# Two weight tiles of each SwiGLU's second product, loaded some steps of the program sooner

## The chip, the cores and the metric

The kernel runs on one core of a Trainium2 chip. The metric is the device time of one execution in microseconds (us), shown as the median of three runs. Engines are named as the profile names them: PE is the matrix engine (PEld its weight loads), DVE the vector engine, ACT the scalar engine, SP the engine that issues nearly all DMAs here, in one queue and in order. A DMA that waits on SP holds back all DMAs behind it.

## What is computed

One layer of an encoder on x of 1024 tokens by 1024 features, all float32:

```
h = x + 0.5 * SwiGLU_1(RMSNorm(x))                 # SwiGLU(u) = (silu(u W_gate) * (u W_up)) W_out
u = RMSNorm(h); [q|k|v|g|p|gates] = u W_in         # retention branch and pooling branch
h = h + (sum of gated branches) W_o
h = h + 0.5 * SwiGLU_2(RMSNorm(h))
out = RMSNorm(h)
```

Each SwiGLU has 2816 hidden features. Its first product (to gate and up) and its second (W_out) stand back to back; the change lies where the second begins. There are two such places, one for each SwiGLU.

## The kernel before

**Arithmetic.** Each float32 operand is split in two rounded parts (L161 on ACT makes the high part, L162 on DVE the rest), and each product is three matmuls (`mm3`, L181 to L183). On top of that both SwiGLU products run as Strassen products over 2x2 blocks: seven block products instead of eight, with sums and differences of blocks made on DVE.

**Names.** `ffn_in` is the first product: tiles named a in SwiGLU 1 and c in SwiGLU 2. `a_ra` and `a_rb` are raw weights, `a_S`, `a_wS`, `a_wL`, `a_wx` and the like are combinations of them and their split forms, `a_a`, `a_b`, `a_e`, `a_x`, `a_y` are PSUM banks, `ag` and `au` the gate and up tiles. `ffn_out` is the second product: tiles named b in SwiGLU 1 and d in SwiGLU 2. It runs over k = 0 to 10, pairs of hidden blocks. For each k its first step p1(k) loads `r` (hidden rows that the first product stored, shown as `br<-r`), `ra` (a 512 KB row of W_out, shown as `bra<-in_f_out`) and for two k at a time the block `bL22a`. Step p6(k) makes three sums of weight blocks on DVE: `s1 = L21 + L22` (L906), `s2 = s1 - L11` (L907), `s3 = L11 - L21` (L908). All three read `ra`.

**Order of the work.** The kernel is one stream of steps, each a preparation (loads and splits) and a body (matmuls). `Flow.run` calls a step's preparation four steps (`LOOK`) ahead of its body. Work that has no place of its own (scaling by the norm, silu, stores of hidden tiles) goes into a queue, `flow.back`; after each body the next one or two pieces of that queue are taken (`flow.rate`). A scheduler under this then sets each engine's order. So while the last two groups of `ffn_in` are still on PE, the first steps of `ffn_out` already stand among them on DVE, ACT and SP.

**Buffers.** `ra` for k below 4 comes from `wide`, a pool of 28 buffers ("mv") which also holds the normed input in split form, n1 or n3, the moving operand of `ffn_in`. Such a buffer comes free when the last matmul that reads its operand is done. `ra` for k from 4 comes from `raw`, four buffers shared with the raw weights of `ffn_in`.

**At the end of ffn_in.** The last two groups share part of their seventh of the products through `common` (L576 onwards): `one`, `two` and `three` multiply halves of blocks into the bank `a_x` and others. Before `three` PE must wait for DVE: L619 reads `a_x` into `ag`, and only then may the matmuls of `three` add on to the same bank.

Of the kernel before, what the change touches and what calls it, by code (L numbers as in the profile page):

```python
# [18 lines left out]
S = 1024  # L19
# [34 lines left out]
BY_OPERAND = (0, 4, 1, 3, 2, 6, 5)  # L54
# [36 lines left out]
def block_kernel(ctx: ExitStack, tc, x, x_tok, x_two, vecs, f1_in, f1_out, w_in, w_v, pool_w, w_ret, w_pool, w_o,  # L91
# [25 lines left out]
    def wide(name):  # L117
        return sb.tile([P, S], F32, tag="mv", bufs=N_MV, name=name)
# [4 lines left out]
    def tl(name):  # L123
        return sb.tile([P, S], F32, tag="tl", bufs=N_TL, name=name)
# [4 lines left out]
    def c2(name):  # L129
        return sb.tile([P, H], F32, tag="c2", bufs=N_C2, name=name)  # L130
# [4 lines left out]
    def sum_bank(name):  # L135

        return ps.tile([P, H], F32, tag="sum", bufs=N_SUM, name=name)

    def load(dst, src):
        nc.sync.dma_start(dst, src)  # L140
# [8 lines left out]
    def half(t, j):  # L149
        return t[:, j * H : (j + 1) * H]  # L150
# [67 lines left out]
    for n in range(N_SUM):  # L218
        b = sum_bank(f"set{n}")
# [77 lines left out]
    class Next(Norm):  # L297
# [24 lines left out]
        def g(self, mt, v=None):  # L322
            if self.gain is None:
                return None
            v = vec if v is None else v
            return v[:, self.gain + mt : self.gain + mt + 1]
# [307 lines left out]
    def parted(steps, between):  # L634

        return steps[0], steps[1], between, steps[2]
# [14 lines left out]
    def then(step, work):  # L651


        def body():
            step[1]()
            flow.add(*work)

        return step[0], body

    def pairs_of_both(nx, groups, first, some):  # L660

        groups = list(groups)
        A, B = (g(()) for g in groups[:2])
        steps = [g[m] for m in first for g in (A, B)]
        n = 2
        if len(groups) % 2:
            C = groups[n](())
            steps += [C[m] for m in BY_SUM]
            n += 1
        tl_, t4_ = ("tl", N_TL), ("t4", N_T4)  # L670

        steps[-1] = then(steps[-1], nx.blocks("R22", [t4_, tl_, t4_], True))
        yield from steps
        for k, n in enumerate(range(n, len(groups), 2)):
            A, B = (g((2, 3) if k >= some else (3,)) for g in groups[n : n + 2])
            yield A[0]
            yield B[0]
            if k < some:
                yield A[4]
                yield then(B[4], nx.blocks("R21", [tl_] * 3, True)) if k == some - 1 else B[4]  # L680
            if k > some:
                yield from parted(common(nx, A, B, 2), A[3])
            else:
                yield A[3]
            yield from (A[1], B[3], B[1], A[2], B[2])
            if k != some:
                yield from parted(common(nx, A, B, 3), A[6])
                yield B[6]
            else:
                yield from parted(common(nx, A, B, 2), A[6])  # L690
                yield from parted(common(nx, A, B, 3), B[6])
# [46 lines left out]
            yield prep, body  # L738


    def ffn_in(nx, w, ops, name, start=None):

        R, T, B, T4 = ops
        hid = {}

        def group(g):
            gate_up = {}

            def dest(which):
                tile, j = which  # L750
                if tile not in gate_up:
                    gate_up[tile] = (tl if start and g == 0 else t4)(f"{name}{'gu'[tile]}{g}")
                return half(gate_up[tile], j)

            later = []

            def evac(which, in0, in1):
                tile, j = which
                dst, rms = dest(which), nx.rb
                if in1 is not None:  # L760
                    tt(dst, in0, in1, ADD)
                elif not tile and rms is not None:
                    tt(dst, in0, half(rms, j), MUL)
                    return
                else:
                    copy(dst, in0)
                if not tile:
                    later.append(j)

            def end():  # L770
                gate, up = gate_up[0], gate_up[1]

                def scale():
                    if len(later) == 2:
                        tt(gate, gate, nx.rms(), MUL)
                    else:
                        for j in later:
                            tt(half(gate, j), half(gate, j), half(nx.rms(), j), MUL)

                def times(j):  # L780
                    tt(half(up, j), half(gate, j), half(up, j), MUL)

                flow.add(scale, lambda: act(gate, gate, AF.Silu), lambda: times(0), lambda: times(1))
                hid[g] = up
                k = g % FH
                if g < FH:
                    return
                lo, hi, e = hid.pop(k), up, {}
                R11, R12, R21, R22 = half(lo, 0), half(lo, 1), half(hi, 0), half(hi, 1)

                def w1():

                    e["n"], e["m"] = gate, c2(f"{name}m{k}")
                    tt(half(e["n"], 0), R12, R11, SUB)

                def w1b():
                    tt(half(e["n"], 1), R22, R12, SUB)
                    load(B[k], e["n"])

                def w2():  # L800
                    tt(R12, R22, half(e["n"], 0), SUB)
                    load(R[k], lo)
                    load(T[k], hi)

                def w3():
                    tt(e["m"], R21, R12, SUB)
                    load(T4[k], e["m"])
                    done.add(k)

                flow.add(w1, w1b, w2, w3)  # L810

            if start and g == 0:
                return plain_group(nx, start, f"{name}{g}_", evac, end)
            return lambda shared: strassen(nx, w[g, 0], w[g, 1], f"{name}{g}_", evac, end, shared=shared, dest=dest)

        done = ops_done.setdefault(name, set())
        order = [g for k in range(FH) for g in (k, k + FH)]
        if start:

            return chain(group(0), pairs_of_both(nx, (group(g) for g in order[1:]), BY_OPERAND, 3))  # L820
        return pairs_of_both(nx, (group(g) for g in order), BY_OPERAND, 2)


    def plain_group(nx, blocks, name, evac, end):
# [25 lines left out]
    ops_done = {}  # L850


    def ffn_out(nx, ops, ready, w, res, name, sink, end, last=None, beyond=None):

        R, T, B, T4 = ops
# [3 lines left out]
        def rows():  # L861

            t["rb"] = wide(f"{name}rb")
            act(in_row(t["rb"]), in_turns(nx.rms()), AF.Copy, scale=0.5)
# [24 lines left out]
        def p1(k):  # L889
            flow.until(lambda: k in ready)  # L890
            r = tl(f"{name}r{k}")
            load(r, R[k])
            ra = (wide if k < 4 else raw)(f"{name}ra{k}")
            load(ra, w[k, :, :S])
            if k == 6:
                rows()
                for mt in range(KT):
                    acc[mt] = t4(f"{name}acc{mt}")
            t["x"] = half(ra, 0), half(ra, 1), both("L22a", k, lambda z: w[z, :, 2 * H : 3 * H])
            t["r"] = r  # L900
            return half(ra, 0), half(r, 0)
# [45 lines left out]
        ahead = {}  # L947
# [160 lines left out]
    first = Next("n1", V_FFN1)  # L1108
    xt = {mt: t4(f"x{mt}") for mt in range(KT)}
    ra, rb = raw("ra"), raw("rb")  # L1110
    lead = half(ra, 0), half(ra, 1), half(rb, 0), half(rb, 1)
# [28 lines left out]
    ops1 = spill("r", FH), spill("t", FH), spill("b", FH), spill("m", FH, H)  # L1140
    h1, h2 = spill("h1", KT), spill("h2", KT)
# [3 lines left out]
    gates = spill("gt", 2 * KT)  # L1145
    pm, ret = spill("pm", KT), spill("ret", KT)

    def ffn1():
        for n, step in enumerate(ffn_in(first, f1_in, ops1, "a", lead)):
            flow.rate = 1  # L1150
            yield step
        flow.rate = 2
        yield from ffn_out(first, ops1, ops_done["a"], f1_out, x_two, "b", mix.quarter, end1)

    mix = Next("n2", V_MIX, h1)

# [233 lines left out]
    order = [("q", 0), ("k", 0), *(o for pair in zip(heavy, light) for o in pair), *light[len(heavy) :]]  # L1390
# [472 lines left out]
    ffn2 = Next("n3", V_FFN2, h2)  # L1863
    ops2 = spill("r2", FH), spill("t2", FH), spill("b2", FH), spill("m2", FH, H)
# [90 lines left out]
    fin = Last("n4")  # L1955

    def second():
        for n, step in enumerate(ffn_in(ffn2, f2_in, ops2, "c")):
            flow.rate = 1
            yield step  # L1960
        flow.rate = 2
    flow.run(chain(ffn1(), projections(), retention(), merge(), second(),
                   ffn_out(ffn2, ops2, ops_done.setdefault("c", set()), f2_out, h2, "d", fin.quarter, fin.end, fin, f2_far)))
    flow.some(-1)


# [93 lines left out]
```

## Time and profile before

| | |
|---|---|
| median of 3 runs | 2071.99 us (2071.73 to 2072.92) |
| profiled execution | 2071.6 us, of which the span shown by the profile is 2069.8 us |
| PE busy | 2044.7 us, 99% of the span |
| DVE busy | 1835.8 us, 89% |
| ACT busy | 1091.3 us, 53% |
| granted PE clock | 0.999 of full speed on average |
| DMA | 313.57 MB, mean 151 GB/s |

The span leaves 25.1 us in which PE does nothing. Views of the trace give for each instruction its start, its length, and in brackets the idle time before it on its engine with what ended that idle time. Tile names are shown without their numbers, so which `bra` is meant follows from its place in the row of issues.

### The profile page before, as it was taken

Reading aid. Unit: us, or ns where it says so; the run is one execution under the profiler, and the core shown is the slowest. Engines: PE = TensorE matmul, PEld = TensorE weight load, DVE = VectorE, ACT = ScalarE, POOL = GpSimd, SP = SyncE. Lnnn points to the kernel's source line nnn. Section 1 sums busy time; section 2 is a strip of 40 time slices with the busy share of each in tenths; the row PEclk is TensorE's granted clock in tenths of the full one; section 3 lists DMA queues with packets and bytes.
Section 4 is the critical chain, followed back from the end, with each engine's and each line's share of the span. In section 5 each row is a group of like instructions: output and inputs, shape, how many; then the busy total and the mean of one; then the engine's idle time right before and its main releaser. Section 6 shows DMA issues by size and latency. Waiting matters only on the chain.

```text
span 2069.8 us, 29688 instructions
## 1 busy us (share of the span) xinstructions
PE 2044.7 (99%) x10672; PEld 1811.1 (87%) x10672; DVE 1835.8 (89%) x3262; ACT 1091.3 (53%) x2061; POOL 0.2 (0%) x4
## 2 busy tenths in 40 slices
PE   9999999999999999999999999999999999999998
PEld 7888989888888888888888999888789999988887
DVE  8799898998996798999778888999989989899897
ACT  8545444554654535454447763456645545455454
POOL 0000000000000000000000000000000000000000
PEclk9999999999999999999999999999999999999999
DMA  7232424576542323243337566724224232457642
GB/s 263 82 138 77 143 87 142 200 265 203 179 151 94 120 106 130 91 143 120 119 128 236 188 234 235 253 92 162 72 86 137 91 136 87 134 207 267 216 145 100
DMA packets 118819, 313.57 MB, mean 151 GB/s; under 512 B 13200, under 2 KB 17424, under 8 KB 118672
## 3 DMA queue, kind: packets, MB, share of 16 engines
q1 hardware_dynamic: 118096, 310.64, 44.4%
q8 instruction: 83, 1.36, 0.3%
q10 hardware_dynamic: 576, 1.05, 0.1%
q14 instruction: 64, 0.52, 0.1%
HBM read 220.93 MB, written 90.70 MB: 151 GB/s over the span
## 4 chain that ended last, share of the span: by engine, by line
PE 74%; DVE 18%; issue 3%; DMA 3%; ACT 3%; SPq 0%; ACTq 0%; DVEq 0%
PE c_b L181 2%; PE c_b L182 2%; PE c_b L183 2%; PE a_b L181 2%; PE a_b L182 2%; PE a_b L183 2%; PE c_e L183 1%; PE c_e L182 1%; PE c_e L181 1%; PE a_e L181 1%; PE a_e L182 1%; PE a_e L183 1%; PE dp5a L181 1%; PE dp5a L182 1%; PE dp5a L183 1%
## 5 line engine op out<-in xcount | busy, mean ns | idle before, releaser
L182 PE MATMUL c_b<-n3T,c_wS 128*128 128x512 f32 x176 | 66.8, 380 | 0.0
L181 PE MATMUL c_b<-n3T,c_wS 128*128 128x512 f32 x176 | 66.5, 380 | 0.2 <-ACT n3T L161 0.2
L183 PE MATMUL c_b<-n3T,c_wS 128*128 128x512 f32 x176 | 66.7, 379 | 0.0
L181 PE MATMUL a_b<-n1T,a_wS 128*128 128x512 f32 x168 | 63.7, 379 | 0.0
L182 PE MATMUL a_b<-n1T,a_wS 128*128 128x512 f32 x168 | 63.7, 379 | 0.0
L183 PE MATMUL a_b<-n1T,a_wS 128*128 128x512 f32 x168 | 63.7, 379 | 0.0
L181 PE MATMUL a_a<-n1R,a_wL 128*128 128x512 f32 x120 | 45.5, 379 | 0.0
L182 PE MATMUL a_a<-n1R,a_wL 128*128 128x512 f32 x120 | 45.5, 379 | 0.0
L183 PE MATMUL a_a<-n1R,a_wL 128*128 128x512 f32 x120 | 45.5, 379 | 0.0
L182 PE MATMUL c_a<-n3R,c_wL 128*128 128x512 f32 x112 | 42.7, 381 | 1.1 <-DVE n3R L166 1.1
L181 PE MATMUL c_a<-n3R,c_wL 128*128 128x512 f32 x112 | 42.6, 380 | 0.8 <-ACT c_b L521 0.8
L183 PE MATMUL c_a<-n3R,c_wL 128*128 128x512 f32 x112 | 42.5, 379 | 0.0
L181 PEld LDWEIGHTS c_b<-n3T,c_wS 128*128 128x128 f32 x176 | 33.2, 189 | 5.1 <-ACT n3T L161 0.6
L182 PEld LDWEIGHTS c_b<-n3T,c_wS 128*128 128x128 f32 x176 | 33.3, 189 | 4.8 <-DVE n3T L162 0.3
L183 PEld LDWEIGHTS c_b<-n3T,c_wS 128*128 128x128 f32 x176 | 33.3, 189 | 4.6
L162 DVE TENSOR_TENSOR a_wS<-a_S,a_wS 128x512 fp32r<-128x512 f32 x45 | 31.3, 697 | 5.0 <-ACT a_wS L161 4.9
L183 PEld LDWEIGHTS a_b<-n1T,a_wS 128*128 128x128 f32 x168 | 31.8, 189 | 4.5
L182 PEld LDWEIGHTS a_b<-n1T,a_wS 128*128 128x128 f32 x168 | 31.8, 189 | 4.3
L181 PEld LDWEIGHTS a_b<-n1T,a_wS 128*128 128x128 f32 x168 | 31.8, 189 | 4.4
L162 DVE TENSOR_TENSOR c_wS<-c_S,c_wS 128x512 fp32r<-128x512 f32 x46 | 32.0, 698 | 2.4 <-ACT c_wS L161 2.3
L161 ACT CAST c_wS<-c_S 128x512 fp32r<-128x512 f32 x46 | 27.8, 622 | 11.4 <-DVE c_S L484 7.0
L182 PE MATMUL c_e<-n3T,c_wL 128*128 128x512 f32 x88 | 33.5, 380 | 0.1
(3159 smaller groups left out, 8034.8 us busy)
## 6 DMA issues: line engine op xcount, KB each, us to landing
c_ra<-in_f_in SPq DMA_DIRECT2D x22, 512.0 KB, 3.7
c_rb<-in_f_in SPq DMA_DIRECT2D x22, 512.0 KB, 3.8
a_ra<-in_f_in SPq DMA_DIRECT2D x21, 512.0 KB, 3.9
a_rb<-in_f_in SPq DMA_DIRECT2D x21, 512.0 KB, 3.8
t<-au SPq DMA_DIRECT2D x11, 512.0 KB, 2.8
b<-ag SPq DMA_DIRECT2D x11, 512.0 KB, 3.7
r<-au SPq DMA_DIRECT2D x11, 512.0 KB, 3.5
bra<-in_f_out SPq DMA_DIRECT2D x11, 512.0 KB, 5.8
```

Source lines behind the costliest of these rows:

```text
L161: copy(hi, src)
L162: tt(lo, src, hi.bitcast(F32), SUB)
L181: mm(dst, w[0], m[0], start=start, stop=False, skip_group_check=True)
L182: mm(dst, w[0], m[1], start=False, stop=False, skip_group_check=True)
L183: mm(dst, w[1], m[0], start=False, stop=stop, skip_group_check=True)
```

## The change

The loads of `ra` for k = 0 and k = 1 are taken out of p1 and put into a function `fetch_rows`, which is handed to `ffn_in`. In the last pair of groups it is put into the `flow.back` queue after the body of step `B[3]`, the fourth block product of the second group. Eight more steps of `ffn_in` follow before p1(0) of `ffn_out`. Since preparations run four steps ahead, p1(0)'s loads were called before when four more bodies had run, and those of p1(1), two steps behind it, when six had. The loads of k = 2 and later stay where they were.

```diff
-            yield from (A[1], B[3], B[1], A[2], B[2])
+            yield A[1]
+            yield then(B[3], [ahead]) if n == len(groups) - 2 else B[3]
+            yield from (B[1], A[2], B[2])
...
-            ra = (wide if k < 4 else raw)(f"{name}ra{k}")
-            load(ra, w[k, :, :S])
+            if k < 2:
+                ra = fetched[name, k]
+            else:
+                ra = (wide if k < 4 else raw)(f"{name}ra{k}")
+                load(ra, w[k, :, :S])
...
+    fetched = {}
+
+    def fetch_rows(w, name):
+        for k in range(2):
+            r = fetched[name, k] = wide(f"{name}ra{k}")
+            load(r, w[k, :, :S])
...
-        for n, step in enumerate(ffn_in(first, f1_in, ops1, "a", lead)):
+        for n, step in enumerate(ffn_in(first, f1_in, ops1, "a", lambda: fetch_rows(f1_out, "b"), lead)):
...
-        for n, step in enumerate(ffn_in(ffn2, f2_in, ops2, "c")):
+        for n, step in enumerate(ffn_in(ffn2, f2_in, ops2, "c", lambda: fetch_rows(f2_out, "d"))):
```

What this does to each engine is seen in the order of the built program's instructions, which has no times. In these rows tiles carry their k: `bra1` is `ra` of k = 1, `bs10`, `bs20` and `bs30` hold s1, s2 and s3 of k = 0 and 1. In brackets stand the semaphores waited for: `DMAHW0` to `DMAHW7` count earlier DMAs in turn, `PE`, `DVE` and `Activation` count those engines' work.

SP's queue before, SwiGLU 1, from the store of the hidden rows r9 to the load of `bra4`:

```order
L140 DMA r9_133<-au9_3653 128x1024 [waits DMAHW5_49,DVE_49]
L140 DMA bL22a2_4154<-in_f1_out 128x512 [waits DMAHW6_49,Activation_49]
L140 DMA bL22a2_4154<-in_f1_out 128x512 [waits DMAHW7_49]
L140 DMA m9_166<-am9_3916 128x512 [waits DMAHW0_49,DVE_49]
L140 DMA bra1_4101<-in_f1_out 128x1024 [waits DMAHW1_49]
L140 DMA bra2_4152<-in_f1_out 128x1024 [waits DMAHW2_49,PE_49]
L140 DMA br3_4213<-r3_127 128x1024 [waits DMAHW3_49,DVE_49]
L140 DMA br4_4261<-r4_128 128x1024 [waits DMAHW4_49,DVE_49,Activation_49]
L140 DMA bra4_4263<-in_f1_out 128x1024 [waits DMAHW5_49,Activation_49]
```

Here `bra1` waits for no engine of its own account, only for its turn: it stands twelve DMAs behind `bra0`, right behind the store `m9`, which waits for DVE.

SP's queue after, at the place where `bra0` stands in both programs (the two rows ahead of it are the same in both):

```order
L140 DMA a21_rb_3719<-in_f1_in 128x1024 [waits DMAHW4_49,DVE_49]
L140 DMA bra0_4003<-in_f1_out 128x1024 [waits DMAHW5_49,PE_49]
L140 DMA bra1_4005<-in_f1_out 128x1024 [waits DMAHW6_49,PE_49]
L140 DMA br0_4049<-r0_124 128x1024 [waits DMAHW7_49,PE_49]
L140 DMA t9_144<-au20_3670 128x1024 [waits DMAHW0_49,DVE_49]
L140 DMA bL22a0_4051<-in_f1_out 128x512 [waits DMAHW1_49,DVE_49,Activation_49]
```

`bra0` has not moved on SP: it has the same neighbour ahead and the same PE event to wait for as before. `bra1` now stands right behind it and waits for a PE event, the sixth matmul of that block product where `bra0` waits for the third. Further on in SP's queue after:

```order
L140 DMA m9_166<-am9_3916 128x512 [waits DMAHW1_49,DVE_49]
L140 DMA bra2_4152<-in_f1_out 128x1024 [waits DMAHW2_49,PE_49]
L140 DMA br3_4213<-r3_127 128x1024 [waits DMAHW3_49,DVE_49]
L140 DMA bra4_4263<-in_f1_out 128x1024 [waits DMAHW4_49,DVE_49]
L140 DMA bL22a4_4265<-in_f1_out 128x512 [waits DMAHW5_49,DVE_49]
L140 DMA bL22a4_4265<-in_f1_out 128x512 [waits DMAHW6_49]
L140 DMA br4_4261<-r4_128 128x1024 [waits DMAHW7_49,DVE_49]
L140 DMA br5_4310<-r5_129 128x1024 [waits DMAHW0_49,PE_49]
```

`bra2` has moved up to the place that `bra1` held behind `m9`, and `br4` has moved back by three DMAs, behind `bL22a4`.

DVE before, SwiGLU 1, from the split of `a10_wL22` to L619:

```order
L162 TENSOR_TENSOR a10_wL22_3986<-a10_rb_3698,a10_wL22_3986 128x512
L162 TENSOR_TENSOR bp6m1_4132<-br1_4099,bp6m1_4132 128x512
L906 TENSOR_TENSOR bs10_4072<-bra1_4101,bL22a0_4049 128x512
L761 TENSOR_TENSOR au21_4018<-a21_b_3822,a21_p7_3960 128x512
L162 TENSOR_TENSOR a10_wy3_4003<-a21_S2_3876,a10_wy3_4003 128x256
L907 TENSOR_TENSOR bs20_4073<-bs10_4072,bra1_4101 128x512
L908 TENSOR_TENSOR bs30_4074<-bra1_4101 128x512
L162 TENSOR_TENSOR bp1m2_4160<-br2_4150,bp1m2_4160 128x512
L162 TENSOR_TENSOR a21_wL22_4020<-a21_rb_3719,a21_wL22_4020 128x512
L906 TENSOR_TENSOR bs12_4181<-bra2_4152,bL22a2_4154 128x512
L619 TENSOR_TENSOR ag10_3832<-a10_x3_4023,ag21_3833 128x256
```

DVE after, the same stretch (the changed file's lines 763, 911, 912 and 913 are lines 761, 906, 907 and 908 before):

```order
L162 TENSOR_TENSOR a10_wL22_3986<-a10_rb_3698,a10_wL22_3986 128x512
L911 TENSOR_TENSOR bs10_4074<-bra1_4005,bL22a0_4051 128x512
L913 TENSOR_TENSOR bs30_4076<-bra1_4005 128x512
L763 TENSOR_TENSOR au21_4022<-a21_b_3822,a21_p7_3960 128x512
L162 TENSOR_TENSOR a10_wy3_4007<-a21_S2_3876,a10_wy3_4007 128x256
L912 TENSOR_TENSOR bs20_4075<-bs10_4074,bra1_4005 128x512
L162 TENSOR_TENSOR bp6m1_4132<-br1_4101,bp6m1_4132 128x512
L162 TENSOR_TENSOR bp1m2_4160<-br2_4150,bp1m2_4160 128x512
L162 TENSOR_TENSOR a21_wL22_4024<-a21_rb_3719,a21_wL22_4024 128x512
L911 TENSOR_TENSOR bs12_4181<-bra2_4152,bL22a2_4154 128x512
L619 TENSOR_TENSOR ag10_3832<-a10_x3_4027,ag21_3833 128x256
```

The same eleven instructions stand between the same ends: s1 of k = 1 has moved up by one place, s3 by four, and the split of `bp6m1` has moved back by five. On ACT one pair has changed places: the cast of `bp1m2`, which needs the load `br2`, now stands ahead of the cast of `a10_wL22`. PE's order is the same throughout, and so is that of POOL. SwiGLU 2 has the same differences with c and d for a and b. Nothing else in the two programs' orders or waits differs but for which of the eight DMA counters a DMA waits on.

More of the change, by code (lines that the diff above doesn't have):

```diff
@@ L658, in then, with pairs_of_both @@
         return step[0], body
-    def pairs_of_both(nx, groups, first, some):
+    def pairs_of_both(nx, groups, first, some, ahead):
         groups = list(groups)
@@ L738, in plain, with ffn_in @@
             yield prep, body
-    def ffn_in(nx, w, ops, name, start=None):
+    def ffn_in(nx, w, ops, name, ahead, start=None):
         R, T, B, T4 = ops
@@ L818, in ffn_in @@
         if start:
-            return chain(group(0), pairs_of_both(nx, (group(g) for g in order[1:]), BY_OPERAND, 3))
-        return pairs_of_both(nx, (group(g) for g in order), BY_OPERAND, 2)
+            return chain(group(0), pairs_of_both(nx, (group(g) for g in order[1:]), BY_OPERAND, 3, ahead))
+        return pairs_of_both(nx, (group(g) for g in order), BY_OPERAND, 2, ahead)
     def plain_group(nx, blocks, name, evac, end):
@@ L850, in block_kernel, with ffn_out @@
     ops_done = {}
-    def ffn_out(nx, ops, ready, w, res, name, sink, end, last=None, beyond=None):
+    def ffn_out(nx, ops, ready, w, res, name, sink, end, fetched, last=None, beyond=None):
         R, T, B, T4 = ops
@@ L1152, in ffn1 @@
         flow.rate = 2
-        yield from ffn_out(first, ops1, ops_done["a"], f1_out, x_two, "b", mix.quarter, end1)
+        yield from ffn_out(first, ops1, ops_done["a"], f1_out, x_two, "b", mix.quarter, end1, fetched)
     mix = Next("n2", V_MIX, h1)
@@ L1962, in block_kernel @@
     flow.run(chain(ffn1(), projections(), retention(), merge(), second(),
-                   ffn_out(ffn2, ops2, ops_done.setdefault("c", set()), f2_out, h2, "d", fin.quarter, fin.end, fin, f2_far)))
+                   ffn_out(ffn2, ops2, ops_done.setdefault("c", set()), f2_out, h2, "d", fin.quarter, fin.end, fetched, fin, f2_far)))
     flow.some(-1)
```

## The prediction

> **What bounds the kernel now.** I read the page's first part first, then who PE waited for, then the timelines of PE, DVE and SP around the two places that the change touches. Busy time and share of the span come first, then the granted clock in 40 slices:
>
> ```profile
> PE 2044.7 (99%) x10672; PEld 1811.1 (87%) x10672; DVE 1835.8 (89%) x3262; ACT 1091.3 (53%) x2061; POOL 0.2 (0%) x4
> ...
> PEclk9999999999999999999999999999999999999999
> ```
>
> PE has work in 99% of the span at full clock, and the change neither removes nor reorders a matmul. What it can win is idle time of PE: 2069.8 - 2044.7 = 25.1 us in all, so the question is which of these microseconds hang on a weight tile. PE's waits over the whole span, three of 26 rows (us in total, times, longest):
>
> ```profile
> PE wo1b L181 <- ACT wo1wS L161: 1.7, 1, 1.7
> ...
> PE a_x L181 <- DVE ag L619: 1.3, 1, 1.3
> ...
> PE c_x L181 <- DVE cg L619: 1.0, 1, 1.0
> ```
>
> The second and third are the twins: the bank `a_x` (`c_x`) that waits for L619 at the end of the first product of SwiGLU 1 (SwiGLU 2). No row of PE's waits names a tile of the second product itself. PE's timeline there:
>
> ```profile
> 402.46 0.28 PE L183 MATMUL a_b<-n1R22y,a_wy 128*128 128x256 f32 x1
> 404.03 0.38 PE L181 MATMUL a_x<-n1R22y,a_ws 128*128 128x256 f32 x1 [1.29 <-DVE ag L619]
> 404.25 0.28 PE L182 MATMUL a_x<-n1R22y,a_ws 128*128 128x256 f32 x1
> 404.36 0.28 PE L183 MATMUL a_x<-n1R22y,a_ws 128*128 128x256 f32 x1
> ...
> 1852.58 0.28 PE L183 MATMUL c_b<-n3R22y,c_wy 128*128 128x256 f32 x1
> 1853.85 0.38 PE L181 MATMUL c_x<-n3R22y,c_ws 128*128 128x256 f32 x1 [1.00 <-DVE cg L619]
> 1854.07 0.28 PE L182 MATMUL c_x<-n3R22y,c_ws 128*128 128x256 f32 x1
> ```
>
> These half-width matmuls start 0.11 us apart when nothing holds them (404.25 to 404.36). Two places behind 402.46 the second `a_x` would stand at 402.68; it stands at 404.25. So the stall costs PE 1.57 us (the idle 1.29 and a first matmul that pays for its weight load), and the twin 1854.07 - 1852.80 = 1.27. Why is L619 late? DVE's own timeline has one hole ahead of it, and it has a DMA behind it:
>
> ```profile
> 396.30 0.71 DVE L162 TENSOR_TENSOR a_wL<-a_rb,a_wL 128x512 fp32r<-128x512 f32 x1
> 396.90 0.71 DVE L162 TENSOR_TENSOR bp6m<-br,bp6m 128x512 fp32r<-128x512 f32 x1
> 399.01 0.69 DVE L906 TENSOR_TENSOR bs<-bra,bL22a 128x512 f32<-128x512 f32 x1 [1.39 <-DMA bra<-in_f_out]
> 399.61 0.69 DVE L761 TENSOR_TENSOR au<-a_b,a_p 128x512 f32<-128x512 f32 x1
> ...
> 402.95 0.69 DVE L906 TENSOR_TENSOR bs<-bra,bL22a 128x512 f32<-128x512 f32 x1
> 403.56 0.42 DVE L619 TENSOR_TENSOR ag<-a_x,ag 128x256 f32<-128x256 f32 x1
> ...
> 1847.02 0.71 DVE L162 TENSOR_TENSOR dp6m<-dr,dp6m 128x512 fp32r<-128x512 f32 x1
> 1848.83 0.69 DVE L906 TENSOR_TENSOR ds<-dra,dL22a 128x512 f32<-128x512 f32 x1 [1.10 <-DMA dra<-in_f_out]
> ...
> 1853.38 0.42 DVE L619 TENSOR_TENSOR cg<-c_x,cg 128x256 f32<-128x256 f32 x1
> ```
>
> L906 of k = 1 waits for its weight row `bra1`. From there to L619 DVE runs without a hole, one instruction every 0.60 us. So a late load stops DVE, and the ag that PE needs is queued eight instructions behind it. SP's issues say why the load is late:
>
> ```profile
> 373.78 0.33 SPq L140 DMA_DIRECT2D bra<-in_f_out  x1
> 379.28 0.33 SPq L140 DMA_DIRECT2D br<-r  x1
> ...
> 385.02 1.33 SPq L140 DMA_DIRECT2D br<-r  x2
> ...
> 393.44 0.33 SPq L140 DMA_DIRECT2D m<-am  x1
> 393.81 0.92 SPq L140 DMA_DIRECT2D bra<-in_f_out  x2
> 395.24 2.77 SPq L140 DMA_DIRECT2D br<-r  x2
> ...
> 1843.93 0.93 SPq L140 DMA_DIRECT2D dra<-in_f_out  x2
> ```
>
> `bra0` goes at 373.78; `bra1` and `bra2` only at 393.81, as soon as the store `m` is out of the way. `bra1` is there for DVE at 399.01, 5.20 us after its issue (twin: 1848.83 - 1843.93 = 4.90).
>
> **The change part by part.** *The load of k = 0* is not moved at all on SP: same neighbours, same PE event. Worth 0. *The load of k = 1* now stands right behind it and waits for the sixth matmul of a product where `bra0` waits for the third, three matmuls of 0.216 us (spacing of the full-width rows below) later: issue near 374.5, SP free again long before `br0` at 379.28, which waits for a much later PE event. PE's rows there, then stretches of 2 us (last columns: DMA share and GB/s), then the landings of all eleven `bra` and all eleven `br`:
>
> ```profile
> 374.02 0.38 PE L183 MATMUL a_a<-n1R,a_wL 128*128 128x512 f32 x1
> 374.24 0.38 PE L181 MATMUL a_a<-n1R,a_wL 128*128 128x512 f32 x1
> ```
>
> ```profile
> 374.00:376.00 2.00, 2.00 (x13) 1.79 (x12) 2.00 (x4) 0.62 (x1) 0.00 (x0) 1.00 0.57 135
> ...
> 378.00:380.00 2.00, 2.00 (x15) 1.76 (x14) 2.00 (x5) 1.52 (x4) 0.00 (x0) 1.00 0.04 8
> ...
> 394.00:396.00 2.00, 2.00 (x11) 1.73 (x11) 2.00 (x5) 0.73 (x2) 0.00 (x0) 1.00 0.91 227
> ```
>
> ```profile
> DMA to landing us min/median/max: 3.6/5.8/6.6
> ```
>
> ```profile
> DMA to landing us min/median/max: 3.7/5.5/6.6
> ```
>
> Beside `bra0` the DMA engines are all but idle there. Even with the longest landing, 6.6 us, `bra1` is there by 381.1, some 15 us before DVE asks.
>
> *DVE.* Without the hole the eleven instructions run through. L906 of k = 1 takes the slot at 396.90, and counting 0.60 for each full and 0.34 for the half-width split: s3 at 397.50, `au` 398.10, `wy` 398.70, s2 399.04, `bp6m1` 399.64, `bp1m2` 400.24, `wL` 400.84, L906 of k = 2 at 401.44, L619 at 402.04. That is 403.56 - 402.04 = 1.52 us sooner (for the twin 1848.83 - 1847.62 = 1.21). None of these has another input that late: `au` reads a bank whose last matmul starts at 395.75, and the one load left is that of k = 2.
>
> *The load of k = 2* moves into the place of `bra1` at 393.81, with one load less beside it. Even at 6.6 us it lands at 400.41, ahead of 401.44. At the 5.20 of the row it lands at 399.01. So no new hole opens.
>
> *PE.* In the row of before, L619's start and PE's restart are 404.03 - 403.56 = 0.47 apart. So PE can restart at 402.51 where it would be ready at 402.57, with its weight load due 0.11 ahead of that. The stall shrinks to some 0.05 and the gain is DVE's 1.52, below the cap of 1.57. Twin: restart at 1853.38 - 1.21 + 0.47 = 1852.64 against 1852.69, gain 1.21, cap 1.27. Sum 2.73 us. Bounds: nothing at all if DVE's hole only moves, and 2.84 by the caps.
>
> *The load br4* falls back behind `bL22a4`, to DVE's `bp6m1` at 399.64 + 0.70 = 400.34, some 2.7 us later than before (395.24 + 2.77 less its own 0.3). The longest landing of a `br` is 6.6 too, so 407 at the worst. The cast of it:
>
> ```profile
> 393.59 0.62 ACT L161 CAST a_wL<-a_rb 128x512 fp32r<-128x512 f32 x1
> 394.11 0.62 ACT L161 CAST bp1m<-br 128x512 fp32r<-128x512 f32 x1
> ...
> 415.79 0.62 ACT L161 CAST bp1m<-br 128x512 fp32r<-128x512 f32 x1
> ```
>
> (the last row) is 7 us later than that, even after the shift. Cost 0. *The swap on ACT* (the first two rows) puts `bp1m2` at 393.59; its load was issued by 386.35 and its cast of before waited for nothing at 394.11. Cost 0 unless it lands later than 9 us after issue, since DVE reads the cast `a_wL` only at 396.30.
>
> *What follows* hangs on PE, DVE and ACT by events and not by the clock, so the 1.52 us is carried on: after 404 PE has no hole until the branch section, and those name DVE or ACT, whose work moves with it. After 1854 PE's waits have no row at all.
>
> **The rivals.** *(a) The hole only moves.* If `bra2` becomes the late load, DVE stops eight instructions on. For that it must need over 401.44 - 393.81 = 7.6 us; the longest row is 6.6. In the extreme L906 of k = 2 stays at 402.95 and the time stays at 2072.0. *(b) The load is not what DVE waits for.* Releasers are inferred; if the hole at 397.60 had another cause than `bra1`, it would stay when the load comes sooner, the change would not do what it says, and the time would be 2072.0 again. Against it: both twins name the load, and both start on time with a load 4.90 to 5.20 us old, within the 3.6 to 6.6 of all eleven. By the Trainium skill (DMA: Bandwidth & Descriptors, Anatomy of one DMA), which fits a DMA of the GpSimd path as 2.0 us plus its bytes at 436 GB/s, a 512 KB load would take 3.2 us as I estimate from that page; `bra1` would have landed at 397.0, ahead of DVE's need at 397.50, and the sum would be 0 rather than 2.73. The trace does not agree for these loads, which go through SP among others at a DMA share of 0.91: none of the eleven took under 3.6. *(c) SP is blocked: slower.* If the early `bra1` had to wait for its buffer at the head of SP's queue, it would hold `br0`, `bL22a0` and everything behind. `br0` goes at 379.28 and is cast at 384.18:
>
> ```profile
> 384.18 0.63 ACT L161 CAST bp1m<-br 128x512 fp32r<-128x512 f32 x1
> ```
>
> A hold of up to 5.5 us (374 to 379.28) costs nothing; beyond it each microsecond delays `br0`, and ACT, where PE's next combinations queue behind that cast. A buffer freed one block product later than named (twelve matmuls, 2.6 us) still costs nothing; one freed at the end of the group (near 396) would hold SP some 17 us, and if half of that reached PE at both places the time would be 2072 + 17 = 2089. By the Trainium skill (Perfetto Trace Analysis, Optimization Strategy) a gap that repeats can mean that buffers ran out; by that rule an earlier call would find no buffer and the sum would be 0 or a loss. The trace does not agree: the hole stands once in each SwiGLU, and the order shows `bra1` waiting for its turn in the queue alone. Against (c) in itself: the PE event that frees the buffer is three matmuls behind that of `bra0`, a row that the trace has at 373.78. *(d) More than the caps.* One 512 KB load less in a stretch where the DMA share is 0.9 could free other loads, but PE shows no further wait there. A gain of 4.5 us, to 2067.5, would need holes elsewhere to close.
>
> **How the numbers follow.** A profiled time of 2071.6 less 2.73 is 2068.9; the profiled execution lies 0.39 under the median 2071.99, so the prediction for the median is 2069.3. A measurement tells about 0.2% from no change, 4.1 us here; the whole gain is 0.13%. So "within 0.2%" is what a forecast of a true gain gives here. Chances: forecast, a gain of 2 to 3 us, 0.78; (a), up to 1.5 us of gain or none, 0.10; (b) 0.03; (c) 0.04; (d) 0.05. The first three lie within 0.2%, 0.91 of all; I give 0.01 of it to a run-to-run step that makes the forecast look faster. So faster 0.06, same 0.90, slower 0.04. The range goes from 2068.0 (the caps, 2.84, off the lowest run 2071.73, and 0.9 for the spread of the runs, 1.2) to 2072.0, no gain at all, as in (a) and (b); outside are (c), (d) and some of the spread.
>
> **What would show it right or wrong.** Right: `bra` issued twice near 374; no DMA row ahead of L906 of k = 1 on DVE; L619 some 1.5 us closer to 396.30; both rows of `a_x` and `c_x` gone from PE's waits or under 0.1 us; PE busy unchanged at 2044.7 and its idle time near 22.4. Wrong: a hole before L906 of k = 2, `br0` issued later than 379.3, ACT waiting for `br` ahead of `a_wL`, or PE's waits in the branches growing by what was won.

## The result, and the profile after

The changed kernel took 2069.19 us (median of 22 runs) against 2071.93 us for the kernel before on the same chip (22 runs): 2.74 us less, a ratio of 0.9986 with a 95% interval of [0.9981, 0.9992]. That is inside the 0.2% that the prediction called no change, though the interval of the ratio lies clear of 1. The time is 0.1 us from the predicted one, which is partly luck, since all runs but one lie between 2067.57 and 2072.35 us. Here and below medians are of all runs, while ratios and intervals leave out the few that took far longer: one of the 22 here, at 0.65 of full clock, took 3059.9 us, and without it the median is 2068.97. The profiled execution has a span of 2068.0 us (before 2069.8). Busy times from its page, the first part:

```profile
span 2068.0 us, 29692 instructions
...
PE 2045.2 (99%) x10672; PEld 1810.6 (88%) x10672; DVE 1835.5 (89%) x3262; ACT 1091.5 (53%) x2061; POOL 0.2 (0%) x4
```

PE is busy for as long as before and idle for 22.8 us instead of 25.1. SP's issues of the kernel after (start, duration on SP, count):

```profile
373.41 0.98 SPq L140 DMA_DIRECT2D bra<-in_f_out  x2
...
392.83 0.33 SPq L140 DMA_DIRECT2D m<-am  x1
393.25 0.38 SPq L140 DMA_DIRECT2D bra<-in_f_out  x1
...
1823.47 0.98 SPq L140 DMA_DIRECT2D dra<-in_f_out  x2
```

Both loads now leave in one go, `bra0` at 373.41 and `bra1` at 374.06 (a row x2 is two issues); the twins leave at 1823.47 and 1824.11. Behind `m`, where `bra1` and `bra2` left together before, `bra2` leaves alone. DVE's timeline of the kernel after at both places; L911 is L906 of the kernel before:

```profile
396.33 0.68 DVE L911 TENSOR_TENSOR bs<-bra,bL22a 128x512 f32<-128x512 f32 x1
...
400.88 0.68 DVE L911 TENSOR_TENSOR bs<-bra,bL22a 128x512 f32<-128x512 f32 x1
401.48 0.41 DVE L619 TENSOR_TENSOR ag<-a_x,ag 128x256 f32<-128x256 f32 x1
...
1846.48 0.68 DVE L911 TENSOR_TENSOR ds<-dra,dL22a 128x512 f32<-128x512 f32 x1
...
1851.62 0.41 DVE L619 TENSOR_TENSOR cg<-c_x,cg 128x256 f32<-128x256 f32 x1
```

No row carries a wait in brackets: k = 1 (396.33) and k = 2 (400.88) start on time, and L619 follows. PE's timeline of the kernel after, where the two stalls stood:

```profile
401.88 0.28 PE L183 MATMUL a_b<-n1R22y,a_wy 128*128 128x256 f32 x1
401.99 0.33 PE L181 MATMUL a_x<-n1R22y,a_ws 128*128 128x256 f32 x1
402.16 0.28 PE L182 MATMUL a_x<-n1R22y,a_ws 128*128 128x256 f32 x1
...
1852.00 0.28 PE L183 MATMUL c_b<-n3R22y,c_wy 128*128 128x256 f32 x1
1852.11 0.35 PE L181 MATMUL c_x<-n3R22y,c_ws 128*128 128x256 f32 x1
1852.30 0.28 PE L182 MATMUL c_x<-n3R22y,c_ws 128*128 128x256 f32 x1
```

The first matmul of `a_x` follows 0.11 us behind the last of `a_b`. To see where PE's time came from I set the start of each of PE's matmuls in the one trace against the same matmul in the other. From the last matmul of `a_b` to the second of `a_x` (402.46 and 404.25 before, 401.88 and 402.16 after) the lead of the kernel after grows from 0.58 to 2.08, by 1.50 us. At the twin it grows from 0.58 to 1.76, by 1.19 us. That is 2.69 us together, nearly the whole of the 2.74 us between the medians. Away from the two places the lead drifts both ways by up to 0.7 us a step (0.69 lost in the first ten us, 0.46 won at 271, 0.69 lost at 552 in a wait of 0.5 us for DVE), which is why the two spans differ by only 1.8 us.

### The profile page after: what moved, and what is told of

It reads as the page before. It is cut to its first block, busy times and chain, and to the rows that moved or that the text cites. A ratio compares the mean times of both kernels' runs of the same rounds, so it can differ in the third digit from the quotient of the medians.

```text
span 2068.0 us, 29692 instructions
## 1 busy us (share of the span) xinstructions
PE 2045.2 (99%) x10672; PEld 1810.6 (88%) x10672; DVE 1835.5 (89%) x3262; ACT 1091.5 (53%) x2061; POOL 0.2 (0%) x4
## 4 chain that ended last, share of the span: by engine, by line
PE 79%; DVE 14%; ACT 3%; issue 2%; DMA 1%; SPq 0%; ACTq 0%; DVEq 0%
PE a_b L181 2%; PE a_b L182 2%; PE a_b L183 2%; PE c_b L181 2%; PE c_b L182 2%; PE c_b L183 2%; PE a_e L181 2%; PE a_e L183 2%; PE a_e L182 2%; PE c_e L183 2%; PE c_e L182 2%; PE c_e L181 2%; PE a_a L182 1%; PE a_a L181 1%; PE a_a L183 1%
## 5 line engine op out<-in xcount | busy, mean ns | idle before, releaser
L181 PE MATMUL c_e<-n3T,c_wS 128*128 128x512 f32 x88 | 33.5, 380 | 0.0
```

The lines of the kernel that those rows point to most:

```text
L181: mm(dst, w[0], m[0], start=start, stop=False, skip_group_check=True)
```

## The experiments

Three theories are tested of why `bra1` was late. **The turn**: it cannot leave before its place in SP's queue, behind `m`, and that leaves too little time. **The traffic**: it leaves among other transfers and they make it slow. **The partner**: what slows it is `bra2`, 0.5 us behind it. In all three a hole ahead of the L906 of k = 1 then reaches PE through L619. Each ratio is against the kernel before, run beside the kernel in question (its medians lie between 2071.94 and 2072.32 us), with a 95% interval. PE's lead is measured as above, from the last matmul ahead of the bank to the second one of the bank. Line numbers differ a little between the kernels: the add that reads `bra` and `bL22a` is L906, L908, L910, L911, L912, L913 or L914.

**Only the k = 1 load moved, and only the k = 0 load.**

```diff
-            if k < 2:
+            if (name, k) in fetched:
...
     def fetch_rows(w, name):
-        for k in range(2):
+        for k in (1,):        # the other kernel: (0,)
```

> Only the load of k = 1 is called early; that of k = 0 stays in p1. On SP the row of bra for k = 1 now stands ahead of that for k = 0, all else as in the changed kernel. Theory (the late load of k = 1 held DVE, and L619 behind it held PE): no hole on DVE ahead of the sums of k = 1, no row of a_x and c_x among PE's waits, the full gain of 2.7 us, some 2069.2. Rival (the pair or the load of k = 0 carries it): a gain clearly smaller, up to 2072.

> Only the load of k = 0 is called early. The order of every engine and every wait are then those of the kernel before, so this is also a second look at that kernel. Theory: DVE's hole of about 1.4 us and its twin of 1.1 are back, PE's stalls at a_x and c_x too, 2072. Rival (calling k = 0 sooner matters in itself): some of the 2.7 us is won.

With k = 1 alone the time was 2068.78 us, ratio 0.9983 [0.9975, 0.9992], and PE's lead jumped by 1.51 and 1.18 us at the two places. DVE's timeline has no wait there:

```profile
396.87 0.72 DVE L911 TENSOR_TENSOR bs<-bra,bL22a 128x512 f32<-128x512 f32 x1
...
1844.64 0.72 DVE L911 TENSOR_TENSOR ds<-dra,dL22a 128x512 f32<-128x512 f32 x1
```

With k = 0 alone it was 2071.39 us, ratio 0.9998 [0.9990, 1.0007], and the holes stood there as before, on DVE's timeline:

```profile
398.58 0.69 DVE L911 TENSOR_TENSOR bs<-bra,bL22a 128x512 f32<-128x512 f32 x1 [1.18 <-DMA bra<-in_f_out]
...
1849.41 0.69 DVE L911 TENSOR_TENSOR ds<-dra,dL22a 128x512 f32<-128x512 f32 x1 [1.15 <-DMA dra<-in_f_out]
```

So the load of k = 1 carries the whole gain. Its neighbour changes nothing: the kernel with k = 0 alone has the program of the kernel before, instruction for instruction.

**The k = 2 load moved as well.**

```diff
-            if k < 2:
+            if k < 3:
...
-        for k in range(2):
+        for k in range(3):
```

> The loads of k = 0, 1 and 2 are called early; otherwise as the changed kernel. Theory: bra for k = 2 already landed in time in the changed kernel, so its early load is worth nothing more: 2069.2 and the same waits. Rival (DMA traffic around 394 to 402 costs something still): up to 1 us more is won, or SP is held at the third buffer and something is lost.

It took 2069.83 us, ratio 0.9989 [0.9981, 0.9998]: no more than the change. In the changed kernel nothing waits for `bra2`, so bringing it sooner wins nothing.

**`m` stored by POOL, so that `bra1` need not wait behind it.** In the kernel before:

```diff
-                    load(T4[k], e["m"])
+                    (nc.gpsimd.dma_start if k == FH - 2 else load)(T4[k], e["m"])
```

> The kernel before, with one store of each SwiGLU (m for k = 9, the one ahead of bra of k = 1 in SP's queue) issued by POOL instead of SP; the loads are called where they were. Theory, queue order: bra for k = 1 waited for its turn behind that store only, so it now leaves right behind the bL22a loads, about 3 us sooner (near 390.6 on the clock of before), lands near 396 and DVE has no hole: full gain, about 2069.2, within 0.7 of the changed kernel. Rival, buffers or DMA traffic: the load stays late although SP is free, hole and time as before, 2072.

A miss for the turn as the prediction had put it: 2072.43 us, ratio 0.9997 [0.9988, 1.0006]. The load left 3.0 us sooner (SP's timeline), took 8.0 us (DMA issues, the last column is us from issue to landing; 5.2 before), and DVE still waited:

```profile
390.81 1.01 SPq L140 DMA_DIRECT2D bra<-in_f_out  x2
```

```profile
bra<-in_f_out SPq DMA_DIRECT2D x1, 512.0 KB, 8.0
```

```profile
398.84 0.69 DVE L906 TENSOR_TENSOR bs<-bra,bL22a 128x512 f32<-128x512 f32 x1 [1.11 <-DMA bra<-in_f_out]
```

But the edit did two more things: `bra2` came forward together with `bra1`, and `m`, by another queue, took 7.2 us instead of 2.1. The next runs take traffic and partner apart.

**Less traffic ahead of `bra1`.** The kernel before, with the second half of `bL22a2` in a tile of its own:

```diff
                 for z in range(at, min(2, FH - k + at)):
-                    load(half(t[key], z), src(k + z - at))
+                    if key != "L22a" or k + z - at != 3:
+                        load(half(t[key], z), src(k + z - at))
+            if key == "L22a" and k == 3:
+                t[key] = raw(f"{name}{key}{k}")
+                load(half(t[key], at), src(k))
```

> The kernel before; of the two halves of the tile bL22a2 (dL22a2) that leave just ahead of the store m, the second, 256 KB, gets a tile of its own and leaves later, behind br3; the loads of bra4, bL22a4 and bra5 follow one buffer later. bra1 keeps its place behind m, and bra2 leaves 0.55 us behind it as before. Theory of the backlog ahead: 256 KB less lie ahead of bra1, at the 355 to 388 GB/s of that stretch 0.68 to 0.74 us, so the holes ahead of L906 shrink from 1.39 and 1.10 to about 0.7 and 0.4, PE's waits at a_x and c_x likewise by 0.7 each, and the time is 1.4 us under the kernel before. Theory of the turn: bra1 still leaves when m does, takes 5.2 and 4.9, holes and time as before. Theory of the pair: what slows bra1 is bra2 beside it, the holes shrink by 0.3 at most.

The traffic theory missed: 2072.28 us, ratio 1.0000 [0.9992, 1.0009], the load took 5.1 us, and the holes were there (DVE's timeline):

```profile
398.48 0.69 DVE L910 TENSOR_TENSOR bs<-bra,bL22a 128x512 f32<-128x512 f32 x1 [1.26 <-DMA bra<-in_f_out]
...
1848.38 0.69 DVE L910 TENSOR_TENSOR ds<-dra,dL22a 128x512 f32<-128x512 f32 x1 [1.21 <-DMA dra<-in_f_out]
```

**The partner held back, for 2 us and until `bra1` has landed.** The kernel before, with a one-column copy on POOL that `bra2`'s load has to wait for:

```diff
+            if k == 2:
+                nc.gpsimd.tensor_copy(ra[:, :1], t["gate"])
             load(ra, w[k, :, :S])
+            if k == 1:
+                t["gate"] = ra[:, :1]     # the first kernel: a column of the k = 1 operand
```

> The kernel before; only the load of k = 2, bra2 (dra2), leaves later: a one-column copy on POOL, which reads the k = 1 operand that DVE writes at 395.10, has to come first, so bra2 should leave near 396.1, behind br3, and not at 394.36, 0.55 us behind bra1. bra1's own place, behind the store m, is as before, and so is everything ahead of it. Theory of the pair: in the kernel before the loads that left at 393.81 and 394.36 took 5.2 and 5.9 us side by side, and in the changed kernel the one that left in the same place without a partner took 3.9 (twin 4.5, against 4.9). So bra1 should take about 3.9 to 4.0 and land near 397.8, DVE's waits ahead of L906 shrink from 1.39 and 1.10 to 0.1 to 0.3 and 0.6 to 0.8, and PE's waits at a_x and c_x from 1.29 and 1.00 to under 0.3 and to 0.5 to 0.7, unless bra2, now late itself (leaving 396.1, 4.3 us, landing 400.4 where DVE would ask at 400.1), opens a hole of 0.3 in its place. Time 0.8 to 1.6 us under the kernel before. Theory of the turn (what counts is when its own issue comes) and theory of the backlog ahead of it: nothing ahead of bra1 differs, so it takes 5.2 (4.9) again, the holes stay 1.39 and 1.10, and the time is that of the kernel before within 0.3 us.

> The kernel before; the load of k = 2, bra2 (dra2), may leave only when bra1 (dra1) has landed: a one-column copy on POOL that reads bra1 stands ahead of it. The program's order follows: DVE takes L910 (L906 before) of k = 2 behind L619 instead of ahead of it, bra4 leaves ahead of bra2, ACT takes bp1w1 two places later. Theory of the sharing, formed from the runs so far: what is outstanding at the same time splits the engines, so a load's time goes by its company over its whole flight. With a partner 0.55 us behind it bra1 or dra1 took 4.9 to 5.2 in six records, with the partner 2.35 us behind 4.8 and 5.1, while bra2 of the changed kernel with only br3 beside it took 3.9 and 4.5. Here only br3, and late in the flight bra4, go beside bra1: 3.9 to 4.6 us, the holes ahead of L910 of k = 1 fall from 1.39 and 1.10 to 0.1 to 0.7. L619 comes 0.6 us sooner by the order alone, so PE's waits at a_x and c_x fall under 0.2, and the time is 1.5 to 2.7 us under the kernel before, less what bra2, which now lands near 402 to 403, costs at its new place behind L619 (0 to 1 us each). Theory of a fixed time (a load of these rows at this place takes 4.9 to 5.2 whatever its company): the holes stay at 1.1 to 1.4, PE's waits fall by the 0.6 of the order alone to 0.7 and 0.4, the time is 0.9 to 1.2 us under the kernel before.

With `bra2` held back to 395.91 the time was 2071.82 us, ratio 1.0000 [0.9991, 1.0009], and `bra1` and `dra1` took 4.8 and 5.1 us. DVE's timeline:

```profile
398.43 0.69 DVE L908 TENSOR_TENSOR bs<-bra,bL22a 128x512 f32<-128x512 f32 x1 [1.07 <-DMA bra<-in_f_out]
...
1847.91 0.69 DVE L908 TENSOR_TENSOR ds<-dra,dL22a 128x512 f32<-128x512 f32 x1 [1.30 <-DMA dra<-in_f_out]
```

With `bra2` held back until `bra1` had landed it was 2071.12 us, ratio 0.9996 [0.9987, 1.0005], and the two loads took 4.5 and 5.9 us. DVE's timeline:

```profile
398.78 0.69 DVE L910 TENSOR_TENSOR bs<-bra,bL22a 128x512 f32<-128x512 f32 x1 [0.75 <-DMA bra<-in_f_out]
...
1850.15 0.69 DVE L910 TENSOR_TENSOR ds<-dra,dL22a 128x512 f32<-128x512 f32 x1 [2.08 <-DMA dra<-in_f_out]
```

With nobody beside it but `br3` and, late, `bra4`, one load was quicker than before and its twin slower. **A partner added** to `bra2` of the changed kernel:

```diff
                 load(ra, w[k, :, :S])
+            if k == 2:
+                load(wide(f"{name}more"), w[1, :, :S])
```

> The changed kernel plus one more load of 512 KB from the same weights (k = 1's rows again, into a tile that nothing reads) right behind bra2 (dra2); PE's and DVE's instructions stand in the same order. One look, to measure bra2's time. Theory of the sharing: bra2, which took 3.9 and 4.5 us in the changed kernel and 3.8 in its second profile, takes 4.9 to 5.2 us with a partner 0.55 us behind it, the partner about 5.8, and br3 behind them 6.1 instead of 4.4. It lands at 398.2 to 398.5, before DVE asks at 400.88, so no hole, and PE's time is the changed kernel's. Theory of the turn or of bytes ahead: nothing ahead of bra2 differs, it takes 3.8 to 4.5.

One execution took 2067.54 us. `bra2` took 4.1 us and `dra2` 4.5 (DMA issues), as without a partner (3.9 and 4.5):

```profile
bra<-in_f_out SPq DMA_DIRECT2D x1, 512.0 KB, 4.1
```

```profile
dra<-in_f_out SPq DMA_DIRECT2D x1, 512.0 KB, 4.5
```

With these two the partner theory, and the sharing that I had made of it (4.9 to 5.2 us forecast for `bra2` with a partner), fell for loads that leave behind `m`.

**The early loads asked for one more step sooner.** The changed kernel, and in it

```diff
-            yield B[0]
+            yield then(B[0], [ahead]) if n == len(groups) - 2 else B[0]
...
-            yield then(B[3], [ahead]) if n == len(groups) - 2 else B[3]
+            yield B[3]
```

> The changed kernel with the early loads asked for one more step of the program sooner (behind the fifth instead of the eighth step of the last pair). The instructions stand in the same order on every engine and wait for the same things, since the buffers come free no sooner, so it is a second profile of the changed kernel: bra0 and bra1 leave near 373.4, no wait ahead of L911, a_x and c_x gone from PE's waits, 2.4 to 3.0 us under the kernel before. It also shows which of the steps in PE's time away from the two places (up to 0.7 us) repeat; a step that does not repeat is from run to run and not the change's. A theory in which the place of the call in the program counts by itself would have a further gain here, 0.3 us or more over the changed kernel.

It took 2070.15 us, ratio 0.9988 [0.9978, 0.9997]; the rows of `a_x` and `c_x` behind L619 were gone again, and PE's lead jumped by 1.48 and 1.19 us there. The step of 0.69 us at 552 became 0.18, so it was not the change's. And `bra2` alone took 3.8 us in SwiGLU 1 and `dra2` 6.1 in SwiGLU 2 (DMA issues), against 3.9 and 4.5 for the same program before: one load at one place varies by 1.6 us from one execution to the next.

```profile
dra<-in_f_out SPq DMA_DIRECT2D x1, 512.0 KB, 6.1
```

**1 MB more traffic in the changed kernel, ahead of `bra2`.**

```diff
                     load(T4[k], e["m"])
+                    if k == FH - 2:
+                        for z in range(4):
+                            load(extra[z], e["m"])
...
+    extra = spill("ex", 4, H)
```

> The changed kernel plus four extra stores of 256 KB each (the tile that m stores, to scratch space that nothing reads) in SP's queue right behind m, ahead of bra2, in both SwiGLUs. PE's, ACT's and DVE's work is the same, DVE's in the same order; br4 leaves two places sooner. It asks whether a late load just ahead of L619 costs PE its full length again. bra2 leaves some 1.4 us later than 393.25, near 394.7, with 1 MB more in the rings; DVE asks for it at 400.88 without a wait in the changed kernel. If the extra 1 MB counts in full at 350 to 400 GB/s (2.6 to 3.0 us) bra2 lands 394.7 + 3.9 + 2.6 to 3.0 = 401.2 to 401.6, a hole of 0.3 to 0.7 ahead of L911 of k = 2, and PE's wait at a_x comes back with 0.2 to 0.7, the time 0.4 to 1.4 us over the changed kernel. If only the turn counts, bra2 lands at 394.7 + 3.9 to 5.2 = 398.6 to 399.9, no hole, and the time is the changed kernel's. In either case each 1 us of hole at L911 of k = 2 should show as 0.9 to 1.1 us at a_x; a hole without a PE wait would say that PE's wait has another cause.

It took 2068.87 us, ratio 0.9985 [0.9976, 0.9994]. `bra2` left at 395.30, 2.05 us later than in the changed kernel and so even later than I had it, took 4.9 us, and DVE found it there at 400.93; no hole came back, so the run says nothing on how a hole there reaches PE.

**`bra1` ahead of `m` in SP's own queue.** The kernel before, with the load of k = 1 asked for in the step before (`early()` takes the tile and loads it):

```diff
+            ra = t.pop("early", None) if k == 1 else None
+            if ra is None:
...
+            if k == 0:
+                early()
             return s2, half(t["r"], 1)
```

> The kernel before; only the load of k = 1, bra1 (dra1), is asked for in the step of the second product ahead of its own, and stands in SP's queue ahead of the store m instead of behind it: it should leave at about 390.6, 3.2 us sooner, m and bra2 behind it as before (the run with m on POOL sent bra2 off together with bra1 and stored m through another queue, this one does neither). DVE takes L906 of k = 1 one instruction (0.60 us) sooner, with the displaced one behind it, the same work in all ahead of L619; DVE so asks for bra1 at 397.0. bra4 leaves ahead of br4. The records so far give 3.8 to 6.1 us for this load or its like from 393.1 to 394.4, and 8.0 and 7.8 from 390.8. Theory of the slack (the wait is the load's time less what the program leaves between its issue and L906, which grows from 3.8 to 6.4 us here): with the usual 3.8 to 6.1 us bra1 lands by 396.7, no hole, a_x and c_x gone from PE's waits, 2.2 to 2.8 us under the kernel before, as much as the move by twenty us. Theory of the busy stretch (a load that leaves between 386 and 393 cannot land before about 398, since the engines were busy 0.95 to 1.10 of the time there with loads that had left before it): 7.5 to 8.2 us, landing 398.1 to 398.8, holes of 1.1 to 1.8 at the new place, less than 0.4 us of time gained or lost.

It took 2070.71 us, 1.6 us under the kernel before beside it, ratio 0.9993 [0.9984, 1.0002]. That interval does not exclude no change, so what was won has to be read from the traces. SP's timeline and DVE's:

```profile
389.84 0.56 SPq L140 DMA_DIRECT2D bra<-in_f_out  x1
392.79 0.33 SPq L140 DMA_DIRECT2D m<-am  x1
...
1839.37 0.49 SPq L140 DMA_DIRECT2D dra<-in_f_out  x1
```

```profile
396.29 0.68 DVE L912 TENSOR_TENSOR bs<-bra,bL22a 128x512 f32<-128x512 f32 x1
...
401.43 0.42 DVE L619 TENSOR_TENSOR ag<-a_x,ag 128x256 f32<-128x256 f32 x1
...
1846.49 0.69 DVE L912 TENSOR_TENSOR ds<-dra,dL22a 128x512 f32<-128x512 f32 x1 [0.78 <-DMA dra<-in_f_out]
```

In SwiGLU 1 the load took 5.9 us of the 6.45 it had, the hole is gone, and PE's lead jumps by 1.54 us, all of what the change wins there. In SwiGLU 2 it took 7.1 us of 6.34, a hole of 0.78 is left, and 0.56 us is won. The theory of the slack holds at the first place and in part at the second; the busy stretch's landing near 398 did not come, though its slower loads did. The run answers one more rival, that the gain comes from DVE's new order: DVE takes its instructions here in the very order of the changed kernel, and where the load is late PE waits all the same, 0.44 us.

## Why the prediction was right

The records of this load where it leaves late, with those of the changed kernel beneath, say together what the wait is. "Slack" is the time from the load's issue to the moment DVE asks (the start of the add less its wait):

| kernel | slack, us | load took, us | hole, us |
|---|---|---|---|
| before | 3.81; 3.80 | 5.2; 4.9 | 1.39; 1.10 |
| k = 0 alone (same program) | 3.80; 3.8 | 5.0; 4.9 | 1.18; 1.15 |
| less traffic ahead | 3.82; 3.8 | 5.1; 5.0 | 1.26; 1.21 |
| partner 2 us later | 3.80; 3.8 | 4.8; 5.1 | 1.07; 1.30 |
| partner after landing | 3.81; 3.80 | 4.5; 5.9 | 0.75; 2.08 |
| `m` by POOL | 6.92; 6.96 | 8.0; 7.8 | 1.11; 0.87 |
| ahead of `m` | 6.45; 6.34 | 5.9; 7.1 | 0; 0.78 |
| after | 22.3; 22.4 | 5.2; 4.2 | 0; 0 |

The hole is the load's time less the slack, to within the rounding, in every row where the load is the longer, and nothing where the slack is. And the slack is fixed by the program wherever the load leaves behind `m`: `m` waits for DVE's `am`, the load goes right behind it, and DVE reaches L906 a fixed run of instructions after `am`, so 3.8 us however the runs differ. The ten records of `bra1` and `dra1` in that place are all longer, 4.5 to 5.9 us.

By the prediction's own steps:

- *PE is busy 99%; only its idle time can be won.* Right: busy 2044.7 before and 2045.2 after, idle 25.1 and 22.8 (22.4 forecast).
- *The stalls at `a_x` and `c_x` hang on L619, and L619 on the hole.* Right, and by experiment: PE's waits behind L619 at the two places go with the holes, 1.29 and 1.00 (holes 1.39, 1.10), 1.0 and 0.8 (1.11, 0.87), 1.2 and 1.1 (1.26, 1.21), 0.9 and 1.1 (1.07, 1.30); with no hole there is no row. With `bra1` ahead of `m` a hole of 0.78 left a wait of 0.4. In the run with the partner held back to the landing DVE had one add less ahead of L619, 0.60 us, and PE waited 1.4 for a hole of 2.08 and had no row for one of 0.75.
- *Size: 1.52 and 1.21 us, capped at 1.57 and 1.27.* Right, and closely: 1.50 and 1.19 in the changed kernel, 1.48 and 1.19 in its second profile, 1.51 and 1.18 with k = 1 alone. L619 was forecast at 402.04; it stands at 401.48, and all but 0.02 us of that is the 0.58 us of lead that PE had already.
- *The load of k = 0 is worth nothing.* Right, as its own run shows.
- *The load of k = 1 leaves near 374.5 and lands by 381.1.* Right: it left at 374.06, 0.65 us behind `bra0`, and took 5.2 us.
- *`bra2` takes its place and lands by 400.41, in time.* Right: issued at 393.25 it took 3.9 us. Its longest record in that place was 6.7 (the run ahead of `m`), under the 7.6 from which rival (a) would have decided.
- *"`bra1` waits only for its turn."* Right as to what sets its issue, and too simple as to what that is worth. The two runs that let it go some 3.1 to 3.3 us sooner (against the `bL22a` issues ahead of it) won very different amounts. With `m` on POOL the holes shrank by 0.3 and 0.2 us; ahead of `m` the whole was won at one place and about half at the other. The load took 8.0 and 7.8 us in the first, 5.9 and 7.1 in the second, against 5.2 and 4.9 behind `m`. In the first `bra2` came along and `m` went by another queue; which of the two cost the load more was not tested. The change moved it by twenty, into a stretch where it had 22 us, and so its time no longer counted. Had it moved by three, the longest landing of 6.6 us on which my sum relied would have been too short.
- *br4 later and the swap on ACT cost nothing.* Right as far as the trace shows: no row of PE's waits names them.
- *The rivals.* (b), that DVE waits for something else, is refuted by the table (DVE asked at 397.62, 399.01 less the 1.39, a little later than the prediction has it). (c), SP blocked, did not come: `br0` left at 378.70. (d) did not come in the medians. The Trainium skill's fit for a DMA of the GpSimd path (DMA: Bandwidth & Descriptors, Anatomy of one DMA), by which I had estimated 3.2 us for such a load, stays below every record of these loads here, from 3.5 in an idle stretch to 10.0 in a busy one with 1 MB of stores added.

What sets the time of a load that leaves behind `m`, between 3.8 and 6.7 us, stays open. 256 KB less ahead of it, a partner removed, a partner added and 1 MB of stores ahead moved it by no more than the 1.6 us by which two executions of one program differ for `dra2`. That is a wide yardstick: `bra2` alone took 3.9, 4.0 and 3.8 us in three runs, and 4.9 with the stores ahead. One lead nobody followed is the row that is loaded. At the early place the load that went first took 3.5 to 3.8 us in all 24 records in which it was that of k = 0, and 4.4 us in both in which it was that of k = 1.

## What to carry to other kernels

Judge a late load by its slack, from its issue to the moment its reader asks, against the longest record of that load and not its median; an in-order queue in which it stands behind a store that waits for compute ties the issue to that compute, and the slack to a few instructions. Move it to a place where the slack is far above any record: here moves by more than twice the wait stayed in the same busy stretch, and one of them won little. And read what the move is worth from the matmul it ends at, since two profiles of one program can differ elsewhere by much of this gain: between the kernel before and the run with k = 0 alone the lead moved by some 2 us.

## What the runs showed of the hardware that I had not expected

In the second profile of the changed kernel PE waited 2.05 us for `vL11w` near 608 to 610, where the kernel before waited 1.52. Then its matmuls started 0.43 us apart instead of 0.22 until 613.95, and its lead over the kernel before fell from 1.39 to -0.28 us, on top of the 0.53 of the longer wait; by 621 it was back at 0.46. The windows of that profile (width, busy PE, PEld, DVE, ACT, POOL, PE's granted clock, DMA share, GB/s):

```profile
608.00:610.00 2.00, 0.40 (x2) 0.00 (x0) 2.00 (x4) 0.17 (x1) 0.00 (x0) 1.00 0.00 0
610.00:612.00 2.00, 1.55 (x4) 1.28 (x5) 2.00 (x4) 0.45 (x1) 0.00 (x0) 0.64 0.00 0
612.00:614.00 2.00, 2.00 (x7) 1.55 (x6) 2.00 (x5) 1.10 (x2) 0.00 (x0) 0.50 0.17 68
614.00:616.00 2.00, 2.00 (x11) 1.76 (x10) 2.00 (x5) 2.00 (x5) 0.00 (x0) 1.00 0.51 195
```

The granted clock fell to 0.50 and came back within 4 us. It fell to 0.50 again at 1396 in the same profile, behind waits of 1.68 and 0.45 us close together that were as long in the kernel before, where the matmuls behind them kept their 0.22 us. So the length of the wait alone does not decide. The second dip cost 0.67 us of lead, so two such dips can hide most of a gain of this size in a single profile. The Trainium skill (TensorE: Matmul & The Clock Gate, Part 1: The HAM clock gate) says that the clock is gated by activity in a free-running window of some 3.4 us, with 426.7 ns from one matmul of 512 columns to the next at half clock; the spacing of 0.43 us agrees, and a window that runs free would let one wait dip in one execution and not in another. Its rule that half clock comes behind an idle window of about 3.4 us does not fit: waits of 2.05 us, and of 1.68 and 0.45 us close together, were enough here.
